# A gated convolution MLP on one core: part of the down projection by seven block products instead of eight

## The chip, the core and the metric

The kernel runs on one core of a Trainium2 chip. The metric is device time of one execution in microseconds. A core has TensorE (PE, matmuls; its weight loads are listed as PEld), VectorE (DVE), ScalarE (ACT), GpSimd (POOL) and SyncE (SP), each working through its own instruction stream, and 16 DMA engines that move data between device memory and the core's SBUF. Matmul results land in PSUM, eight banks of 128 partitions x 512 floats.

## The reference

One layer of a decoder trunk on 256 tokens with 2048 columns, in float32: an attention mixer (latent attention and sliding-window attention, gated and merged), then a gated MLP with a causal convolution of width 3. The change is in the MLP:

```python
D_MODEL = 2048; SEQ = 256; D_FF = 5632; CONV_WIDTH = 3

def conv_ffn(h, w_up, conv_w, conv_b, w_down):
    S = h.shape[1]
    a, b = jnp.split(h @ w_up, 2, axis=-1)
    ap = jnp.pad(a, ((0, 0), (CONV_WIDTH - 1, 0), (0, 0)))
    c = conv_b
    for j in range(CONV_WIDTH):
        c = c + conv_w[j] * ap[:, j:j + S]
    return (jax.nn.gelu(c, approximate=True) * b) @ w_down

x = x + rms_norm(hybrid_mixer(rms_norm(x, norm_mix_pre), ...), norm_mix_post)
x = x + rms_norm(conv_ffn(rms_norm(x, norm_ffn_pre), ...), norm_ffn_post)
```

The down projection is (256 x 5632) times (5632 x 2048).

## The kernel before, in words

**Three matmuls for one.** Every float32 operand is held as a high and a low part, each in the matmul's reduced float format. A product is three matmuls: high x high, high x low, low x high (`mm3`, lines 163 to 166). A matmul has a 128 x 128 stationary operand, here the activations of one ktile (128 values of the inner dimension) and one row tile (128 of the 256 tokens), and a moving operand of up to 512 weight columns.

**How weights come in.** `wchunk` (lines 116 to 140) fetches 512 KB of weights from SP's queue into a raw buffer of 128 x 1024 floats, which is one column block of 512 for two ktiles. ACT then casts it to the high part (line 138), and DVE subtracts to get the low part (line 139). There are three raw buffers in this part of the kernel (`RAW = 3`) and five slots for high and low parts (`RING = 4` and one extra pair that the `flex` buffers supply). `gemm` (lines 168 to 188) loops over the chunks of one column block: two ktiles x two row tiles x three matmuls, 12 matmuls a chunk.

**What sets the order.** The program is written in one order, and small pieces of other work (transposes, gate columns, loads) are put between the chunks with `at(t, f)`: f is written out when the counter `now`, which `tick()` moves on by one a chunk, reaches t. A planner then fixes each engine's order: it takes ready work in the program's order of rank and moves work up where an engine would be idle. It also gives out buffers: a tile of a tag with n buffers waits until the n-th before it is done with.

**The MLP.** The 44 ktiles of the inner dimension D_FF come in 11 column blocks of 512. Block 0 is made by `ffn_up0`, blocks 1 to 10 by `ffn_up` (lines 1007 to 1028): 16 chunks, eight for the activation half into the four PSUM banks of pool `pacc`, eight for the gate half into the four banks of pools `pss` and `pst`. Their results are brought into SBUF by ACT and DVE (`evac`, lines 1011 to 1019), and four `conv_cols` (lines 912 to 926), written among the first seven chunks of what follows, do the convolution, the gelu and the gate, and leave the ktile's 256 tokens as high and low parts (`GH`, `GL`). There is room for 24 ktiles of these. So the down projection has two parts: after block 5 the first 24 ktiles (lines 1036 to 1044), one column block of 512 after the other, each with 12 chunks, into two PSUM banks, which ACT and DVE then copy to `dsum`. Blocks 6 to 10 follow, then the second part with 20 ktiles (lines 1085 to 1106), which adds its results to `dsum`, takes the norm and (`finish`, lines 1071 to 1083) adds x2, the residual stream, in SBUF since the mixer, and stores the output, row tile 0 in four pieces and row tile 1 in five.

**Memory.** x2 lies in SBUF from the mixer's end to the last addition, in two tiles of 128 x 2048 floats (tags `x2_0`, `x2_1`). The results of `evac` lie in tiles of 128 x 512, four each of tags `fa` and `fb`.

Of the kernel before, what the change touches and what calls it, by code (L numbers as in the profile page):

```python
# [19 lines left out]
P = 128  # L20
# [21 lines left out]
def trunk_layer(ctx, tc, x, x_cols_in, conv_cols_in, g_mix_post, g_ffn_post, w_in, w_q, w_kv,  # L42
# [16 lines left out]
    def sb(pl, shape, name, dt=F32, tag=None, bufs=None):  # L59
        return pl.tile(shape, dt, name=name, tag=tag or name, **({"bufs": bufs} if bufs else {}))  # L60
# [55 lines left out]
    def wchunk(src, shape, own=None, rawp=None, rbufs=1, parts=None):  # L116
        i = cnt[0]
        cnt[0] += 1
        n = int(np.prod(shape))
        raw = rawp.tile([P, 1024], F32, name=f"raw{i}", tag="xraw", bufs=rbufs) if rawp else \  # L120
            ring_tile("raw", f"raw{i}", F32, in_turn("raw"))
        dst = raw[:, :n]
        if len(shape) == 2:
            dst = dst.rearrange("p (a b) -> p a b", a=shape[0])
        elif len(shape) == 3:
            dst = dst.rearrange("p (a b c) -> p a b c", a=shape[0], b=shape[1])
        if len(shape) == 3:
            for k in range(shape[0]):
                nc.sync.dma_start(dst[:, k], src[:, k])
        else:  # L130
            nc.sync.dma_start(dst, src)
        if own:
            hi, lo = (own.tile([P, 1024], F32R, name=f"w{part}{i}", tag="w" + part) for part in ("hi", "lo"))
        else:
            extra = in_turn("w")
            hi, lo = (ring_tile("w" + part, f"w{part}{i}", F32R, extra) for part in ("hi", "lo"))
        for a, b in parts or ((0, n),):
            act.copy(hi[:, a:b], raw[:, a:b])  # L138
            vec.tensor_tensor(lo[:, a:b], raw[:, a:b], hi[:, a:b].bitcast(F32), op=ALU.subtract)  # L139
        return hi, lo  # L140


    steps = defaultdict(list)
    now = [0]

    def at(t, *fs):
        steps[max(t, now[0])].extend(fs)
# [444 lines left out]

    ta_d = dram.tile([4, NT, P, 512], F32, name="ta_d")
    yb_d = dram.tile([4, NT, P, 512], F32, name="yb_d")

    def gate_b(j):
        acc, _ = gemm(XH, XL, w_in, 0, KT, C_GB + 512 * j, 512)
# [233 lines left out]
            at(now[0] + (3 if j == 3 else 1) + p, lambda p=2 * j + p, ld=ld: m_cols(p, ld))  # L831


    yg = [[sb(p6, [P, 512], f"yg_{t}_{j}", tag="f" + "ab"[t], bufs=4) for j in range(4)] for t in range(NT)]
# [114 lines left out]
    def ffn_up0():  # L949

        sa = [[None, None], [None, None]]

        def evac(acc, q):
            for t in range(NT):
                a = sb(p6, [P, 512], f"f{q}_0_{t}", tag="f" + "ab"[q], bufs=4)
# [51 lines left out]
    def ffn_up(c, slot0):  # L1007

        sa = [[], []]

        def evac(acc, q):
            for i in range(4):
                if i % 2 == 0:
                    f = sb(p6, [P, 512], f"f{q}_{c}_{i}", tag="f" + "ab"[q], bufs=4)
                a = f[:, (i % 2) * 256:(i % 2) * 256 + 256]
                sc = (1.0, 0.5)[q]
                act.activation(a, acc[i][:, 256:512], AF.Copy, scale=sc)
                vec.scalar_tensor_tensor(a, acc[i][:, 0:256], sc, a, op0=ALU.mult, op1=ALU.add)
                sa[q].append(a)

        acc = [pacc.tile([P, 512], F32, name=f"ua{c}_{i}", tag="acc") for i in range(4)]
        gemm_cols(acc, 512 * c)
        evac(acc, 0)
        acc = [(pss, pst)[i // 2].tile([P, 512], F32, name=f"ub{c}_{i}", tag="st"[i // 2]) for i in range(4)]
        gemm_cols(acc, DFF + 512 * c)
        evac(acc, 1)
        for i in range(4):
            at(now[0] + 1 + 2 * i, lambda i=i: conv_cols(4 * c + i, sa[0][i], sa[1][i], slot0 + i))
# [2 lines left out]
    gpost2 = sb(p6, [P, D], "gpost2", tag="gp")  # L1031
    pool.dma_start(gpost2, g_ffn_post.partition_broadcast(P))
    for c in range(1, 6):
        ffn_up(c, 4 * c)

    def down(k0, nk, c0, n, split=None, ps=None):
# [34 lines left out]
    def finish(t):  # L1071
        v, y, w, r = (sb(p3, [P, 1], f"{n}z{t}") for n in "vywr")
        q = ssz[t][:, NB - 1:NB]
        act.activation(y, q, AF.Sqrt, scale=1.0 / D, bias=zpre[t])
        vec.tensor_scalar(v, q, -0.5 / D, zneg[t], op0=ALU.mult, op1=ALU.add)
        vec.reciprocal(y, y)

        vec.scalar_tensor_tensor(w, v, y[:, 0:1], y, op0=ALU.mult, op1=ALU.mult)
        vec.scalar_tensor_tensor(r, w, 1.5, y, op0=ALU.add, op1=ALU.mult)
        cuts = (0, 256, 768, 1280, 1792, 2048) if t else (0, 512, 1024, 1536, 2048)  # L1080
        for a, b in zip(cuts[:-1], cuts[1:]):
            vec.scalar_tensor_tensor(dsum_all[t][:, a:b], dsum_all[t][:, a:b], r[:, 0:1], x2_all[t][:, a:b], op0=ALU.mult, op1=ALU.add)
            nc.sync.dma_start(out[t * P:(t + 1) * P, a:b], dsum_all[t][:, a:b])
# [104 lines left out]
```

## Time and profile before

| | |
|---|---|
| median of 3 runs | 1477.52 us (1477.09 to 1478.06) |
| the profiled execution, its time | 1477.15 us |
| its span, first to last instruction | 1475.4 us |
| mean granted TensorE clock | 0.998 |
| blocks 1 to 5 of the up projection | 44.5 us each |
| first part of the down projection | 1004.45 to 1135.01 us of the span |
| bytes read from device memory | 275.69 MB |

How to read the rows: a group row is "line engine operation output<-input shape xcount | busy us in all, mean ns of one | idle us of the engine before them, and what ended most of it". Tile names leave their numbers out: `whi` and `wlo` are the weights' high and low parts, `raw` the raw buffer, `accg` a PSUM bank of a `gemm`, `ua` and `ub` the banks of an up block, `ghl` and `bhl` the activations' parts, `ds` the tile of `dsum`. A row of the list of waits is "who, line <- for whom, line: us in all, times, longest". A row of a timeline is "start, duration, engine, line, operation, x count, idle time before it". Lines of helpers (138, 139, 164 to 166, 219, 220) serve many stages.

### The profile page before, as it was taken

To read this page: it belongs to the slowest core of one execution; us is meant where nothing else is said; L and a number is where in the kernel's file an instruction comes from. 1 tells how busy PE (TensorE), PEld (TensorE's weight loads), DVE (VectorE), ACT (ScalarE), POOL (GpSimd) and SP (SyncE) were. 2 spreads that over 40 slices of the span, in tenths; PEclk is the share of its full clock that TensorE was granted. 3 is DMA by queue.
4 is the path that set the end of the run, shared out by engine and by line. 5 is a ranking of instruction groups with operands and counts; after the bars stand their busy time and mean duration, and the time that the engine had idled before them with its cause. 6 is when DMAs were issued, how large, how long until landed. Compare 5 with 4: busy or idle time off the path is not lost.

```text
span 1475.4 us, 20769 instructions
## 1 busy us (share of the span) xinstructions
PE 1464.5 (99%) x7615; PEld 1251.1 (85%) x7615; DVE 979.7 (66%) x1716; ACT 806.2 (55%) x1336; POOL 46.8 (3%) x79
## 2 busy tenths in 40 slices
PE   9999999999999999999999999999999999999997
PEld 7888888888888888888888888888888888888886
DVE  7788874445667665555799677675444676677556
ACT  7588864444565554444666565564444555465443
POOL 0022100000000010000000000000000000000000
PEclk9999999999999999999999999999999999999999
DMA  8755376666655559656656666665656666666663
GB/s 291 219 174 165 94 216 198 204 210 200 186 159 156 171 164 340 223 193 200 194 177 180 197 189 186 189 195 187 198 190 197 188 187 195 188 186 189 197 191 123
DMA packets 159010, 283.40 MB, mean 192 GB/s; under 512 B 18187, under 2 KB 29612, under 8 KB 158780
## 3 DMA queue, kind: packets, MB, share of 16 engines
q1 hardware_dynamic: 154800, 268.34, 59.2%
q0 software_dynamic: 4016, 13.68, 3.1%
q8 instruction: 60, 0.98, 0.3%
q14 instruction: 42, 0.34, 0.1%
q10 hardware_dynamic: 92, 0.05, 0.0%
HBM read 275.69 MB, written 6.34 MB: 191 GB/s over the span
## 4 chain that ended last, share of the span: by engine, by line
PE 96%; DVE 2%; ACT 1%; DMA 1%; issue 0%; DVEq 0%; SPq 0%
PE accg L164 18%; PE accg L166 18%; PE accg L165 18%; PE ub L995 10%; PE ua L995 10%; PE ub L999 5%; PE ua L999 5%; PE mpo L748 1%; PE ms L714 1%; DMA raw<-in_w_in_dram 1%; PE pt L431 1%; PE qn L679 1%; PE qn L677 1%; PE qn L678 1%; PE s L451 0%; PE ms L719 0%
## 5 line engine op out<-in xcount | busy, mean ns | idle before, releaser
L139 DVE TENSOR_TENSOR wlo<-raw,whi 128x1024 fp32r<-128x1024 f32 (+2 forms) x502 | 609.5, 1215 | 404.5 <-ACT whi L138 395.0
L138 ACT CAST whi<-raw 128x1024 fp32r<-128x1024 f32 (+2 forms) x502 | 523.0, 1044 | 513.8 <-PE accg L166 300.8
L164 PE MATMUL accg<-whi,bhl 128*128 128x512 f32 x570 | 222.8, 391 | 0.0
L166 PE MATMUL accg<-whi,bhl 128*128 128x512 f32 x570 | 222.1, 390 | 0.0
L165 PE MATMUL accg<-wlo,bhl 128*128 128x512 f32 x570 | 222.0, 389 | 0.0
L164 PE MATMUL accg<-whi,ahl 128*128 128x512 f32 (+1 forms) x544 | 212.9, 391 | 0.0
L166 PE MATMUL accg<-whi,ahl 128*128 128x512 f32 (+1 forms) x544 | 210.5, 387 | 0.0
L165 PE MATMUL accg<-wlo,ahl 128*128 128x512 f32 (+1 forms) x544 | 209.7, 385 | 0.0
L995 PE MATMUL ua<-ahl,whi 128*128 128x512 f32 x640 | 154.6, 391 | 0.0
L995 PE MATMUL ub<-ahl,whi 128*128 128x512 f32 x640 | 154.5, 391 | 0.0
L995 PEld LDWEIGHTS ub<-ahl,whi 128*128 128x128 f32 x640 | 117.5, 188 | 22.9 <-ACT cc L917 0.2
L995 PEld LDWEIGHTS ua<-ahl,whi 128*128 128x128 f32 x640 | 117.5, 188 | 22.7
L166 PEld LDWEIGHTS accg<-whi,bhl 128*128 128x128 f32 x570 | 107.0, 188 | 22.3
L164 PEld LDWEIGHTS accg<-whi,bhl 128*128 128x128 f32 x570 | 107.0, 188 | 22.0
L165 PEld LDWEIGHTS accg<-wlo,bhl 128*128 128x128 f32 x570 | 107.0, 188 | 21.8
L166 PEld LDWEIGHTS accg<-whi,ahl 128*128 128x128 f32 x544 | 102.1, 188 | 20.4
L165 PEld LDWEIGHTS accg<-wlo,ahl 128*128 128x128 f32 x544 | 102.3, 188 | 18.1
L164 PEld LDWEIGHTS accg<-whi,ahl 128*128 128x128 f32 x544 | 102.3, 188 | 18.0
L999 PEld LDWEIGHTS ub<-ahl,wlo 128*128 128x128 f32 x640 | 82.2, 191 | 3.2
L999 PEld LDWEIGHTS ua<-ahl,wlo 128*128 128x128 f32 x640 | 82.2, 191 | 3.1
L999 PE MATMUL ua<-ahl,wlo 128*128 128x256 f32 x640 | 83.7, 283 | 0.0
L999 PE MATMUL ub<-ahl,wlo 128*128 128x256 f32 x640 | 83.2, 283 | 0.0
(359 smaller groups left out, 1586.5 us busy)
## 6 DMA issues: line engine op xcount, KB each, us to landing
raw<-in_ffn_w_up_dram SPq DMA_DIRECT2D x176, 512.0 KB, 4.4
raw<-in_w_in_dram SPq DMA_DIRECT2D x111, 512.0 KB, 4.5
raw<-in_ffn_w_down_dram SPq DMA_DIRECT2D x88, 512.0 KB, 3.8
raw<-in_w_o_swa_dram SPq DMA_DIRECT2D x32, 512.0 KB, 4.3
raw<-in_w_o_mla_dram SPq DMA_DIRECT2D x32, 512.0 KB, 4.7
raw<-in_w_out_dram SPq DMA_DIRECT2D x32, 512.0 KB, 4.2
bias<-strip POOLq DMA_DIRECT2D x16, 256.0 KB, 4.4
raw<-in_mla_w_q_up_dram SPq DMA_DIRECT2D x32, 128.0 KB, 2.4
```

What stands on the lines that cost most here:

```text
L138: act.copy(hi[:, a:b], raw[:, a:b])
L139: vec.tensor_tensor(lo[:, a:b], raw[:, a:b], hi[:, a:b].bitcast(F32), op=ALU.subtract)
L164: pe.matmul(o, ah, bh, start=start, stop=False)
L165: pe.matmul(o, ah, bl, start=False, stop=False)
L166: pe.matmul(o, al, bh, start=False, stop=stop)
L431: pe.transpose(pt[:, j * P:(j + 1) * P], p[:, c * P:(c + 1) * P], ident)
L677: pe.matmul(o, wh, ch(k), start=k == 0, stop=False)
L678: pe.matmul(o, wh, cl(k), start=False, stop=False)
L679: pe.matmul(o, wl, ch(k), start=False, stop=k == nk - 1)
L714: pe.matmul(o, w, v_, start=n == 0, stop=False)
L995: pe.matmul(acc[i], hi[:, c], hn[p][:, j * 512:(j + 1) * 512], start=p + j == 0, stop=stop)
L999: pe.matmul(acc[i][:, 0:256], lo[:, c], hn[p][:, j * 512:j * 512 + 256], start=False, stop=False)
```

## The change

The first part of the down projection takes two column blocks (1024 columns) at a time, in two halves p = 0 and 1 (`down_pair`), and its ktiles in pairs. A pair, with two row tiles of tokens and two column blocks, is a product of 2 x 2 blocks: eight block products. For pairs 0 to 3 it is done with seven, in Winograd's form of Strassen's method, from sums of blocks: four sums of activation blocks (`token_sums`, made once, used in both halves) and four sums of weight blocks (`ta`, `tb`, made in each half). Pairs 4 to 11 stay plain. The order in a half is `psppsppsppsp` (p plain, s seven).

Each weight row of 128 x 1024 is fetched whole into a raw buffer (`raw_row`); `convert` is the cast and the subtraction of `wchunk`, on their own. A plain pair converts two chunks of 1024. A seven-block converts the odd row (1024), half of the even row (512), `ta` and `tb` (1024 each). Seven products need seven accumulators beside the plain fourth: four banks c11, c12, c21, c22 take what goes to one result block alone, four banks q1, q5, q7, q6 what goes to several; all eight banks are used. After the last seven-block the q banks go into `dsum` by one copy and four additions, and at the half's end the four c banks are added.

The activation sums need room: x2 is stored to device memory (`park`, eight pieces from POOL's queue, written among the chunks of up block 2), its two tiles hold the sums, and x2 is fetched back (`unpark`, eight pieces from SP's queue, placed 40 chunks after the first part). The `fa`/`fb` tiles become 128 x 1024, two of each tag, so that `ta` and `tb` fit in them. Row tile 1 of the output is stored in four pieces of 512, as row tile 0.

```diff
+    def convert(raw, n, own=None, parts=None):
+    def raw_row(src):
+        raw = ring_tile("raw", f"raw{i}", F32, in_turn("raw"))
+        nc.sync.dma_start(raw, src)
+        return raw
...
+    x2_d = dram.tile([NT, P, D], F32, name="x2_d")
...
+    yg_all = [[sb(p6, [P, 1024], f"yg_{t}_{j}", tag="f" + "ab"[t], bufs=2) for j in range(2)] for t in range(NT)]
...
+    def park(t, j):
+        pool.dma_start(x2_d[t, :, j * 512:(j + 1) * 512], x2[t][j])
+
+    def unpark(t, j):
+        if j == 0:
+            x2_all[t] = sb(p3, [P, D], f"x2b_{t}", tag=f"x2_{t}")
+        c = slice(j * 512, (j + 1) * 512)
+        nc.sync.dma_start(x2_all[t][:, c], x2_d[t, :, c])
+
+    def token_sums(u):
+        if u % 2 == 0:
+            s_tiles.append(sb(p3, [P, D], f"s_{u // 2}", F32R, tag=f"x2_{u // 2}"))
+        hi, lo = (s_tiles[u // 2][:, (u % 2) * 1024 + i * 512:(u % 2) * 1024 + (i + 1) * 512] for i in range(2))
+        g = gtiles[u].bitcast(F32)
+        a, m = (sb(s_pool[0], [P, 512], f"s{n}{u}", tag="hx", bufs=2) for n in "am")
+        vec.tensor_tensor(a, g[:, 0:512], g[:, 512:1024], op=ALU.add)
+        a11, a21, a12, _ = (a[:, i * P:(i + 1) * P] for i in range(4))
+        m1, m2, m3, m4 = (m[:, i * P:(i + 1) * P] for i in range(4))
+        vec.tensor_tensor(m1, a21, a[:, 384:512], op=ALU.add)
+        vec.tensor_tensor(m3, a11, a21, op=ALU.subtract)
+        vec.tensor_tensor(m2, m1, a11, op=ALU.subtract)
+        vec.tensor_tensor(m4, a12, m2, op=ALU.subtract)
+        split_to(hi, lo, m)
+        s_of[u] = [[x[:, i * P:(i + 1) * P] for x in (hi, lo)] for i in range(4)]
...
     for c in range(1, 6):
+        if c == 2:
+            for i in range(8):
+                at(now[0] + i, lambda i=i: park(i // 4, i % 4))
+        if c == 4:
+            for u in range(4):
+                at(now[0] + 3 + 3 * u, lambda u=u: token_sums(u))
         ffn_up(c, 4 * c)
...
-    for j in range(4):
-        acc, _ = down(0, 24, 512 * j, 512, ps=(pss, "s") if j == 3 else None)
-        for t in range(NT):
-            vec.tensor_copy(dsum[t][j], acc[t]) if t else act.copy(dsum[t][j], acc[t])
+    def banks(kind, name):
+        return [(pacc if kind == 0 else (pss, pst)[i // 2]).tile([P, 512], F32, name=f"{name}{i}", tag="acc" if kind == 0 else "st"[i // 2])
+                for i in range(4)]
+
+    def down_pair(p):
+        c11, c12, c21, c22 = c = banks(p, f"c{p}_")
+        q1, q5, q7, q6 = q = banks(1 - p, f"q{p}_")
+        j0, used = 2 * p, set()
+        d = [dsum[t][j0 + j] for t in range(NT) for j in range(2)]
...
+        def mul(o, x, w, last=False):
+            mm3(o, *x, *w, id(o) not in used, last)
+            used.add(id(o))
+
+        def plain(u, last):
+            for k in (2 * u, 2 * u + 1):
+                w = convert(raw_row(row(k)), 1024)
+                for t in range(NT):
+                    for j in range(2):
+                        mul(c[2 * t + j], act_of(k, t), half(w, j), last and k % 2 == 1)
+                tick()
+
+        def seven(u, last):
+            s1, s2, s3, s4 = s_of[u]
+            even, odd = raw_row(row(2 * u)), raw_row(row(2 * u + 1))
+            ta, tb = (sb(p6, [P, 1024], f"t{n}{p}_{u}", tag="f" + n, bufs=2) for n in "ab")
+            lo_, hi_ = slice(0, 512), slice(512, 1024)
+            w = convert(odd, 1024)
+            vec.tensor_tensor(ta[:, lo_], even[:, hi_], even[:, lo_], op=ALU.subtract)
+            vec.tensor_tensor(ta[:, hi_], odd[:, hi_], even[:, hi_], op=ALU.subtract)
+            vec.tensor_tensor(tb[:, lo_], odd[:, hi_], ta[:, lo_], op=ALU.subtract)
+            vec.tensor_tensor(tb[:, hi_], odd[:, lo_], tb[:, lo_], op=ALU.subtract)
+            mul(c11, act_of(2 * u + 1, 0), half(w, 0))
+            mul(c12, s4, half(w, 1))
+            w = convert(even, 512)
+            mul(q1, act_of(2 * u, 0), half(w, 0), last)
+            w = convert(ta, 1024)
+            mul(q5, s1, half(w, 0), last)
+            mul(q7, s3, half(w, 1), last)
+            tick()
+            w = convert(tb, 1024)
+            mul(q6, s2, half(w, 0), last)
+            mul(c21, act_of(2 * u + 1, 1), half(w, 1))
+            tick()
+            if last:
+                act.copy(d[0], q1)
+                vec.tensor_tensor(d[1], d[0], q6, op=ALU.add)
+                vec.tensor_tensor(d[2], d[1], q7, op=ALU.add)
+                vec.tensor_tensor(d[3], d[2], q5, op=ALU.add)
+                vec.tensor_tensor(d[1], d[1], q5, op=ALU.add)
+
+        plain_of, seven_of = iter(range(4, 12)), iter(range(4))
+        for i, kind in enumerate(PAIR_ORDER):
+            if kind == "s":
+                u = next(seven_of)
+                seven(u, u == 3)
+            else:
+                plain(next(plain_of), i == len(PAIR_ORDER) - 1)
+        for o, x in zip(d, c):
+            vec.tensor_tensor(o, o, x, op=ALU.add)
+
+    for p in range(2):
+        down_pair(p)
+    for i in range(8):
+        at(now[0] + 40 + 2 * i, lambda i=i: unpark(i // 4, i % 4))
     for c in range(6, 11):
         ffn_up(c, 4 * (c - 6))
...
-        cuts = (0, 256, 768, 1280, 1792, 2048) if t else (0, 512, 1024, 1536, 2048)
+        cuts = range(0, D + 1, 512)
...
+PAIR_ORDER = "psppsppsppsp"
```

More of the change, by code (lines that the diff above doesn't have):

```diff
@@ L131, in wchunk @@
             nc.sync.dma_start(dst, src)
+        return convert(raw, n, own=own, parts=parts)
+    def convert(raw, n, own=None, parts=None):
+        i = cnt[0]
+        cnt[0] += 1
         if own:
@@ L140, in wchunk @@
         return hi, lo
+    def raw_row(src):
+        i = cnt[0]
+        cnt[0] += 1
+        raw = ring_tile("raw", f"raw{i}", F32, in_turn("raw"))
+        nc.sync.dma_start(raw, src)
+        return raw
     steps = defaultdict(list)
@@ L831, in trunk_layer @@
             at(now[0] + (3 if j == 3 else 1) + p, lambda p=2 * j + p, ld=ld: m_cols(p, ld))
-    yg = [[sb(p6, [P, 512], f"yg_{t}_{j}", tag="f" + "ab"[t], bufs=4) for j in range(4)] for t in range(NT)]
+    yg_all = [[sb(p6, [P, 1024], f"yg_{t}_{j}", tag="f" + "ab"[t], bufs=2) for j in range(2)] for t in range(NT)]
+    yg = [[yg_all[t][j // 2][:, (j % 2) * 512:(j % 2 + 1) * 512] for j in range(4)] for t in range(NT)]
     blocks = [(0, 512), (512, 512), (1024, 512), (1536, 256), (1792, 256)]
@@ L953, in evac @@
         def evac(acc, q):
+            f = sb(p6, [P, 1024], f"f{q}_0", tag="f" + "ab"[q], bufs=2)
             for t in range(NT):
-                a = sb(p6, [P, 512], f"f{q}_0_{t}", tag="f" + "ab"[q], bufs=4)
+                a = f[:, t * 512:(t + 1) * 512]
                 act.activation(a, acc[t], AF.Copy, scale=rf[t][q][:, 0:1])
@@ L985, in ffn_up0 @@
             at(now[0] + w, lambda i=i: cols(i))
-        return es7
+        gtiles[:] = g
+        s_pool.append(p7)
+        return es7
+    gtiles, s_pool, s_of = [], [], {}
+    def park(t, j):
[5 more added lines that the diff above has]
+        nc.sync.dma_start(x2_all[t][:, c], x2_d[t, :, c])
+    s_tiles = []
+    def token_sums(u):
[13 more added lines that the diff above has]
+        s_of[u] = [[x[:, i * P:(i + 1) * P] for x in (hi, lo)] for i in range(4)]
     def gemm_cols(acc, c0):
@@ L1011, in evac @@
         def evac(acc, q):
+            f = sb(p6, [P, 1024], f"f{q}_{c}", tag="f" + "ab"[q], bufs=2)
             for i in range(4):
-                if i % 2 == 0:
-                    f = sb(p6, [P, 512], f"f{q}_{c}_{i}", tag="f" + "ab"[q], bufs=4)
-                a = f[:, (i % 2) * 256:(i % 2) * 256 + 256]
+                a = f[:, i * 256:i * 256 + 256]
                 sc = (1.0, 0.5)[q]
@@ L1039, in down @@
         return gemm(xh, xl, w_down, k0, nk, c0, n, split=split, ps=ps)
-    for j in range(4):
-        acc, _ = down(0, 24, 512 * j, 512, ps=(pss, "s") if j == 3 else None)
-        for t in range(NT):
-            vec.tensor_copy(dsum[t][j], acc[t]) if t else act.copy(dsum[t][j], acc[t])
+    def banks(kind, name):
[6 more added lines that the diff above has]
+        d = [dsum[t][j0 + j] for t in range(NT) for j in range(2)]
+        act_of = lambda k, t: (GH(k)[:, t * P:(t + 1) * P], GL(k)[:, t * P:(t + 1) * P])
+        row = lambda k: w_down[k * P:(k + 1) * P, j0 * 512:(j0 + 2) * 512]
+        half = lambda w, i: tuple(x[:, i * 512:(i + 1) * 512] for x in w)
+        def mul(o, x, w, last=False):
[45 more added lines that the diff above has]
+            vec.tensor_tensor(o, o, x, op=ALU.add)
```

## The prediction, made before the change was run

> **What bounds the kernel now.** I read the page first (busy shares, chain), then what TensorE waited for, then the stage of the change.
>
> ```profile
> span 1475.4 us, 20769 instructions
> PE 1464.5 (99%) x7615; PEld 1251.1 (85%) x7615; DVE 979.7 (66%) x1716; ACT 806.2 (55%) x1336; POOL 46.8 (3%) x79
> ...
> PE 96%; DVE 2%; ACT 1%; DMA 1%; issue 0%; DVEq 0%; SPq 0%
> ```
> ```profile
> PE warm L77 <- DVE ramp L66: 1.1, 1, 1.1
> PE pstrip L251 <- DMA sel<-in_strip_sel_dram: 0.5, 1, 0.5
> ```
>
> The second fence is TensorE's whole list of waits, and both are at the start: once going, TensorE is never late by more than a rounding. The chain is TensorE for 96%. A matmul taken out is therefore worth its full pitch, as long as what feeds TensorE keeps up. The pitch comes from the first matmul of the first down part and the first one after it:
>
> ```profile
> 1004.45 0.39 PE L164 MATMUL accg<-whi,bhl 128*128 128x512 f32 x1
> ...
> 1135.01 1.29 PE L995 MATMUL ua<-ahl,whi 128*128 128x512 f32 x5
> ```
>
> Between them lie 4 column blocks x 24 ktiles x 2 row tiles x 3 = 576 matmuls in 130.56 us: 0.2267 us each (the 0.39 of a row overlaps its neighbours and is not the cost). A chunk of weights (one ring slot, 12 matmuls) is 2.72 us, a ktile pair over two column blocks 24 matmuls or 5.44 us.
>
> How far the feed runs ahead is seen in the quiet part of that stage, one conversion on ACT and DVE:
>
> ```profile
> 1015.52 1.05 ACT L138 CAST whi<-raw 128x1024 fp32r<-128x1024 f32 x1 [1.59 <-PE accg L166]
> ```
> ```profile
> 1016.61 1.23 DVE L139 TENSOR_TENSOR wlo<-raw,whi 128x1024 fp32r<-128x1024 f32 x1 [1.39 <-ACT whi L138]
> ```
>
> The cast waited for TensorE to give a slot back: chunk 3 ended at 1004.45 + 4 x 2.72 = 1015.33. There are five slots (RING = 4 and the extra one), so this is chunk 8, which TensorE starts at 1026.2. It is ready at 1017.84, 8.4 us early. That lead is the cover for all that follows.
>
> **What is removed.** In each half (two column blocks) four pairs need 7 products instead of 8: 4 pairs x 2 halves x 3 = 24 matmuls fewer, with their weight loads. 24 x 0.2267 = **5.44 us**. A seven-block has 21 matmuls, 4.76 us. The Trainium skill, "TensorE: Matmul & The Clock Gate", section "Back-to-back issue gap", gives about 131 ns for a 512-column matmul in a stream; by it the sum would be 24 x 0.131 = 3.1 us. The rows of this very stage say 0.2267, and the measurement decides.
>
> **What is added on DVE and ACT in the stage.** Mean durations, of the stage itself and, for shapes it lacks, of the nearest rows elsewhere:
>
> ```profile
> L139 DVE TENSOR_TENSOR wlo<-raw,whi 128x1024 fp32r<-128x1024 f32 x48 | 58.8, 1225 | 63.1 <-ACT whi L138 63.1
> L138 ACT CAST whi<-raw 128x1024 fp32r<-128x1024 f32 x49 | 51.7, 1055 | 70.9 <-PE accg L166 58.0 <-PE accg L165 12.6
> ```
> ```profile
> L722 DVE TENSOR_TENSOR mp<-ms,causal 128x128 f32<-128x128 f32 x16 | 4.6, 286 | 19.6 <-PE ms L719 19.6
> L943 DVE TENSOR_TENSOR hx<-bhl 128x512 f32<-128x512 f32 x8 | 5.4, 683 | 0.0
> ...
> L220 DVE TENSOR_TENSOR ahl<-hx,ahl 128x512 fp32r<-128x512 f32 x8 | 5.3, 683 | 0.0
> L219 ACT CAST ahl<-hx 128x512 fp32r<-128x512 f32 x8 | 4.9, 620 | 3.0 <-DVE hx L945 3.0
> L1055 DVE TENSOR_TENSOR ds<-ds,accg 128x512 f32<-128x512 f32 x6 | 3.8, 679 | 0.0
> ```
>
> A plain pair: 2 subtractions, 2.45 us of DVE for 5.44 of TensorE. A seven-block: 3 conversions of 1024 and one of 512, and four block sums of 512: 3 x 1.225 + 5 x 0.683 = **7.09 us of DVE for 4.76 of TensorE**, and 3 x 1.055 + 0.620 = 3.8 of ACT. So in a seven-block DVE is the slower engine by 2.33 us. In the repeating group (one seven, two plain: 15.64 us of TensorE) DVE has 7.09 + 4.90 = 12.0 us, 77%. On average it fits; the question is whether the lead bridges the block.
>
> A timetable by hand, zero being the start of the two plain pairs ahead of a seven-block (chunks P1 to P4, then O odd row, E even row, T and U the block sums, each in one slot). The slots for O, E, T, U come free at 0, 2.72, 5.44 and 8.16. The rows use three raw buffers, so the odd row is fetched when P3 is converted, at about 0.1, and lands 3.8 us later:
>
> ```profile
> raw<-in_ffn_w_down_dram SPq DMA_DIRECT2D x88, 512.0 KB, 3.8
> ```
>
> O is ready at about 4.5 + 2.3 = 6.8, the first sums at 8.0, the second at 9.2, T at 10.4, U at 11.6. TensorE asks for O at 10.88, E at 12.24, T at 12.92, U at 14.28. The tightest, T and U, are some 2.5 us early. So I expect no wait in the middle of a half. Below, a block could lose nothing; above, with the lead gone, 2.33 us. I take the lower end, because TensorE's list of waits has no entry even where DVE was fuller than here, with 0.3 us in all for eight blocks:
>
> ```profile
> 770.00:780.00 10.00, 10.00 (x46) 8.28 (x45) 9.97 (x14) 5.38 (x7) 0.00 (x0) 1.00 0.71 208
> ...
> 1004.45:1020.77 16.32, 16.32 (x74) 13.51 (x73) 12.25 (x21) 8.90 (x15) 0.00 (x0) 1.00 0.57 190
> 1020.77:1037.09 16.32, 16.32 (x74) 13.51 (x73) 7.35 (x6) 6.81 (x7) 0.00 (x0) 1.00 0.61 194
> ```
>
> (Columns: stretch, PE, PEld, DVE, ACT, POOL busy, clock, DMA share, GB/s.) At 770 DVE is full and PE still 10.00 of 10. The first seven-block comes in the second row's stretch, in which the last gate columns put 12.25 - 7.35 = 4.9 us more on DVE. There the new order has three plain pairs (P, then after the block P, P) and one block: 3 x 2.45 + 7.09 + 4.9 = 19.3 us for 21.1 of TensorE, with four chunks already converted at its start. It fits, more narrowly than the others.
>
> **Results out of PSUM.** Per half, one ACT copy and eight DVE additions (8 x 0.679 = 5.4 us) replace two copies on each; DVE has the room. What waits for them: the four q banks are the next half's c banks, and after the second half the next gate block's. The last seven-block is followed by a plain pair, 5.44 us; from q6's end the evacuation needs 0.6 + 4 x 0.68 = 3.3 us, with one conversion between, 4.5. Hidden; without that pair it would be 3.3 us in each of two places. The c banks have the next half's first pair as cover.
>
> **Block sums of the activations.** Per pair two 512-wide operations, four of 128 and one cast: 2 x 0.683 + 4 x 0.286 = 2.5 us of DVE, 0.62 of ACT; four pairs, 10 us. In the block of columns where they are written, DVE has 44.5 - 31.68 = 12.8 us free and ACT 20:
>
> ```profile
> 915.40:959.90 44.50, 44.50 (x257) 39.35 (x256) 31.68 (x53) 24.08 (x40) 0.00 (x0) 1.00 0.64 189
> ```
>
> They may also go earlier, since the planner pulls ready work ahead: the load of line 1032, written after the first column block, was issued at 738.6. So zero, at worst the 10 us less the lead of 8.4.
>
> **x2 out and back.** Eight stores on POOL's queue, eight loads on SP's, 256 KB each, 4 MB. The rows for one issue on POOL (0.53 us) and one load of x2's size on SP (6.8 us to landing), then a stretch where more of such traffic ran, and what SP waits for in the stage:
>
> ```profile
> L1032 POOL DMA_DIRECT2D gpost<-in_norm_ffn_post_dram x1: 534/534/534, 738.6 to 738.6; - x1
> ```
> ```profile
> x<-in_x_dram SPq DMA_DIRECT2D x8, 256.0 KB, 6.8
> ```
> ```profile
> 560.00:580.00 20.00, 20.00 (x89) 16.54 (x89) 11.41 (x12) 7.79 (x8) 1.08 (x2) 1.00 0.96 341
> ```
> ```profile
> SPq L131 <- DVE wlo L139: 101.9, 45, 2.5
> ```
>
> At 560 the DMA engines were at 0.96 and 341 GB/s and PE had 20.00 of 20, so bursts cost nothing. SP spends 101.9 us of the stage waiting for a raw buffer, so eight more issues find room. A load back waits for the sums' last reader on PE; behind it in SP's queue stand weight rows, and behind these DVE's conversions. It hurts only if it is queued before that reader is done. Fetching weights as whole 4 KB rows moves the same bytes in the same count of loads: no cost.
>
> **The tail.** Each store cut is one DVE operation; four for t = 0 and five for t = 1:
>
> ```profile
> 1462.49 2.74 DVE L1082 SCALAR_TENSOR_TENSOR ds<-ds,rz,x 128x512 f32<-128x512 f32 x4
> ...
> 1468.81 2.87 DVE L1082 SCALAR_TENSOR_TENSOR ds<-ds,rz,x 128x256 f32<-128x256 f32 x5
> ```
> ```profile
> DMA to landing us min/median/max: 1.9/2.4/2.6
> ```
> ```profile
> out_dram<-ds SPq DMA_DIRECT2D x7, 256.0 KB, 2.4
> ...
> out_dram<-ds SPq DMA_DIRECT2D x2, 128.0 KB, 2.2
> ```
>
> Four instead of five saves 0.13 on DVE; the last store is 256 KB, not 128, by the medians 0.2 slower: +0.1 (ends -0.13 and, 1.9 to 2.6, +0.57).
>
> **Sum.** The profiled execution took 1477.15 us (span 1475.4). 1477.15 - 5.44 + 0.3 + 0.1 = 1472.1; the median of the runs is 0.37 above that execution, so **1472.4**.
>
> **Rivals.**
> (1) *The blocks come a little late.* The lead of 2.5 us is worked out with median landings; a DVE queue whose order puts an evacuation or a gate column ahead of T costs 0.4 to 1.0 us a block. For: DVE goes from 47% of the stage (24 x 1.225 + 2 x 0.69 per 65.3) to about 85% (53.4 of 62.6). Against: no wait in the whole run of before. At 0.65 a block in place of the 0.3 in all, 1472.4 - 0.3 + 5.2 = 1477.3, no change.
> (2) *Slower: DVE paces every seven-block.* The sums pin the even and odd raw buffers until the last sum is made, the next rows are fetched late, and the lead doesn't come back in the two plain pairs. Then each block costs its full 2.33 us: 8 x 2.33 = 18.6, so 1477.5 - 5.4 + 18.6 + 0.1 = 1490.8. It decides from 0.67 us a block (break even). Against it: the group's DVE load of 77%.
> (3) *A load of x2 blocks SP.* Queued one group too early, it holds the weight rows for 15.6 us against a lead of 8.4: 7.2 us once, 1479.6, still no change.
> (4) *The matmuls taken out are worth less than their pitch*: at 131 ns each the time is 1474.8. By that rule of the skill; the pitch measured in the stage leaves it next to no chance.
>
> **Chances.** Forecast 0.66 (1471.6 to 1474.5: all blocks hidden, up to 0.3 us each lost). (1) 0.15, (2) 0.13, (3) 0.04, (4) 0.02. A measurement of this kernel tells 0.2%, 3 us, from no change: faster 0.66, same 0.21 (rivals 1, 3, 4), slower 0.13. The range runs from all hidden with the best tail, 1471.5, up through rival 1 to 1478.5, which holds about 8 in 10; the forecast's own is 1471.6 to 1474.5.
>
> **What the profile after would show.** 24 matmuls fewer and 125.1 us instead of 130.6 from the first matmul of the stage to the next gate block; no PE waits there (step "added" right), or waits on the conversions of T and U (rivals 1 and 2), about 0.5 or over 2 us each. DVE at about 85% in the stage. PE waiting at the start of the second half or of the next gate block would show the PSUM step wrong; SP idle on a TensorE releaser, rival 3. PE waiting at 915 to 960 would show the activation sums dear. A pitch other than 0.227 in the seven-blocks would break the first term.

## The result, and the profile after

| | before | after |
|---|---|---|
| median of 20 runs each | 1477.24 us (1476.38 to 1478.21) | 1475.05 us (1473.28 to 1475.86) |
| ratio after / before | | 0.9984, 95% interval 0.9977 to 0.9991 |
| profiled execution: time, span | 1477.15, 1475.4 us | 1475.35, 1473.5 us |
| first matmul of the stage | 1004.45 us | 1003.91 us |
| first matmul of the next gate block (up block 6) | 1135.01 us | 1132.44 us |
| the stage between them | 130.56 us | 128.53 us |
| start of the last matmul to the end of the span | 8.92 us | 8.39 us |

The kernel is faster by 2.2 us. The prediction was 1472.4, a gain of 5.1. The sign is right and the time lies in the whole range (1471.5 to 1478.5), but outside the forecast's own (1471.6 to 1474.5): less than half of the gain came. The page of the profile after:

```profile
span 1473.5 us, 20861 instructions
...
PE 1460.6 (99%) x7591; PEld 1246.1 (85%) x7591; DVE 1026.6 (70%) x1799; ACT 818.3 (56%) x1354; POOL 51.1 (3%) x87
...
PE 92%; DVE 3%; DMA 3%; ACT 1%; issue 0%; DVEq 0%; ACTq 0%; SPq 0%
```

TensorE has 24 matmuls fewer (7615 to 7591), as intended. The last row, the chain, went from 96% on PE to 92%: for some stretch something else sets the end. TensorE's whole list of waits (for whom: us in all, times, longest) says where:

```profile
PE c L176 <- DVE wlo L144: 1.6, 2, 0.8
PE warm L77 <- DVE ramp L66: 1.1, 1, 1.1
PE ua L1041 <- DVE ds L1145: 0.9, 1, 0.9
PE pstrip L262 <- DMA sel<-in_strip_sel_dram: 0.4, 1, 0.4
PE q L176 <- DVE wlo L144: 0.2, 1, 0.2
```

`warm` and `pstrip` are the old waits at the start. New are waits for low parts of weights (`wlo`) in the stage, and one of 0.9 for line 1145, the last addition that takes a q bank out of PSUM. The stage in four parts, two to a half (stretch, PE, PEld, DVE, ACT, POOL busy, clock, DMA share, GB/s):

```profile
1003.91:1035.20 31.29, 31.29 (x140) 25.91 (x139) 24.70 (x35) 16.46 (x23) 0.00 (x0) 1.00 0.57 179
1035.20:1066.47 31.27, 31.27 (x140) 25.89 (x138) 25.34 (x29) 15.96 (x17) 0.00 (x0) 1.00 0.64 202
1066.47:1099.40 32.93, 31.93 (x139) 25.57 (x138) 23.50 (x27) 15.10 (x16) 0.00 (x0) 1.00 0.59 182
1099.40:1132.44 33.04, 32.24 (x140) 25.92 (x139) 24.64 (x27) 16.08 (x18) 0.00 (x0) 1.00 0.69 217
```

The first half takes 62.56 us, which is 276 matmuls x 0.2267: nothing is lost in it. The second half, with the same work, takes 65.97: **3.4 us lost**. With the 0.9 behind it that makes 4.3, where the prediction had 0.3. (The list names 1.8 us in the stage, and these rows show as much idle time, 32.93 - 31.93 and 33.04 - 32.24; the other 1.6 lies in longer steps between matmuls whose ends are modelled, so I go by their starts.) DVE is at 71 to 81% in these rows, so it isn't full. What does set the pace is in the chain of work that ended last, here from the turn of the halves (the end of the first and the start of the second) on (start, duration, what):

```profile
1065.72 0.24 PE c L177
...
1067.20 1.28 DVE ds L1155 x2
1068.47 1.14 DVE wlo L144
...
1070.82 0.60 DVE tb L1126
...
1072.02 0.61 DVE tb L1127
...
1072.65 6.30 DMA raw<-in_ffn_w_down_dram
...
1081.38 5.63 DMA raw<-in_ffn_w_down_dram
...
1087.03 0.69 DVE ta L1125
...
1090.12 3.82 DMA raw<-in_ffn_w_down_dram
...
1096.38 5.74 DMA raw<-in_ffn_w_down_dram
...
1105.80 5.27 DMA raw<-in_ffn_w_down_dram
...
1113.51 6.00 DMA raw<-in_ffn_w_down_dram
...
1122.63 4.02 DMA raw<-in_ffn_w_down_dram
...
1133.54 0.61 DVE ds L1145
...
1134.20 1.42 PE ua L1041 x5
```

Most of the loss can be read in this view. The chain leaves TensorE at 1066, when the first half's last c matmul releases the additions of line 1155. DVE works in order, so the block sums of the second half's first block stand behind these additions. The last sum, at 1072.63, gives a raw buffer back, and from there the chain doesn't return to TensorE until 1134.20: it goes round one raw buffer, load, cast and subtraction (or sums), load again. Six rounds from 1072.65 to 1122.63 take 49.98 us. One buffer of three carries every third row, so six rounds are 18 rows or three groups, for which TensorE needs 3 x 15.64 = 46.92. The difference, 3.06 us, is nearly all of the 3.4 lost. The loads on this chain take 3.8 to 6.3 us, not the 3.8 of the timetable. By the starts of TensorE's matmuls the 3.4 us are lost in two places: 1.8 by 1090, the other 1.6 from 1120.7 on.

What ScalarE waited for in the stage tells the same (before, by the row shown above, it waited for TensorE to give slots back, 58.0 and 12.6 us):

```profile
ACT whi L143 <- DMA raw<-in_ffn_w_down_dram: 52.2, 27, 5.5
...
DVE ta L1125 <- DMA raw<-in_ffn_w_down_dram: 9.4, 6, 2.8
...
ACT whi L143 <- PE c L177: 4.4, 5, 1.5
```

Before, the conversions ran ahead until all slots were full; after, they wait for rows. The stage went from one with a full queue of conversions to one that takes each row as it lands.

### The profile page after: what moved, and what is told of

The parts are those of the page before. It is cut to its first block, busy times and chain, and to the rows that moved or that the text cites. A ratio compares the mean times of both kernels' runs of the same rounds, so it can differ in the third digit from the quotient of the medians.

```text
span 1473.5 us, 20861 instructions
## 1 busy us (share of the span) xinstructions
PE 1460.6 (99%) x7591; PEld 1246.1 (85%) x7591; DVE 1026.6 (70%) x1799; ACT 818.3 (56%) x1354; POOL 51.1 (3%) x87
## 4 chain that ended last, share of the span: by engine, by line
PE 92%; DVE 3%; DMA 3%; ACT 1%; issue 0%; DVEq 0%; ACTq 0%; SPq 0%
PE accg L175 15%; PE accg L177 15%; PE accg L176 15%; PE ub L1041 10%; PE ua L1041 10%; PE ua L1045 5%; PE ub L1045 5%; DMA raw<-in_ffn_w_down_dram 2%; PE c L175 1%; PE c L176 1%; PE c L177 1%; DVE wlo L144 1%; PE mpo L760 1%; PE ms L726 1%; PE pt L442 1%; PE qn L691 1%
## 5 line engine op out<-in xcount | busy, mean ns | idle before, releaser
L175 PE MATMUL accg<-whi,bhl 128*128 128x512 f32 x442 | 173.0, 391 | 0.0
L177 PE MATMUL accg<-whi,bhl 128*128 128x512 f32 x442 | 172.3, 390 | 0.0
L176 PE MATMUL accg<-wlo,bhl 128*128 128x512 f32 x442 | 172.2, 390 | 0.0
L177 PEld LDWEIGHTS accg<-whi,bhl 128*128 128x128 f32 x442 | 83.0, 188 | 17.4
L175 PEld LDWEIGHTS accg<-whi,bhl 128*128 128x128 f32 x442 | 83.0, 188 | 16.9
L176 PEld LDWEIGHTS accg<-wlo,bhl 128*128 128x128 f32 x442 | 83.0, 188 | 16.8
```

The costliest lines, as they stand in the source:

```text
L175: pe.matmul(o, ah, bh, start=start, stop=False)
L176: pe.matmul(o, ah, bl, start=False, stop=False)
L177: pe.matmul(o, al, bh, start=False, stop=stop)
```

## The experiments

**Theory 1**: the three raw buffers are too few for rows that the sums hold longer and that land later; the lead of the feed is used up and can't be won back. **Theory 2**: DVE's load or order (sums, evacuations ahead of conversions). **Theory 3**: the loads of x2, which the planner had moved from 40 chunks behind the stage into its second half (SP issued four of the eight in pairs from 1096.89 and 1101.41, the others after 1131), crowd the weight rows.

A measure for them is the lead of a block: the time from the end of the subtraction that gives the low part of T (U) to the matmul that first reads it (eight, for U two, pitches of 0.2267 before the end of the block's last q matmul). About 0.2 us is the least it can be; there TensorE waits. The stage began between 1003.80 and 1006.58 in the profiled executions, of kernels that are mostly alike up to it. So stages are compared by length, from the first matmul in them to the first of the next gate block, and times by medians. Each ratio is to the kernel before, run on the same chip.

### no_seven: everything but the seven-blocks

```diff
-PAIR_ORDER = "psppsppsppsp"
+PAIR_ORDER = "pppppppppppp"
```

All twelve pairs are plain, c goes straight to `dsum`. The sums of activations, x2 out and back, whole rows and the tail stay.

> The changed kernel with all twelve pairs plain in both halves (576 matmuls, as before the change), so that the activation sums are made but not used, the q banks are not used, and the results are copied out of the c banks. All theories: PE has no wait in the stage, 130.6 us. It shows what the rest of the change costs by itself: against the kernel before, the output tail and nothing else, so 0 to 1 us less. Theory 1 also: whole rows land in about 3.8 to 4.0 us when each buffer is held for a conversion only. If whole rows are slow by themselves, they land in 4.3 or more here too.

1476.84 us (1475.77 to 1477.47), ratio 0.9997 (0.9988 to 1.0006); the stage is 130.56 us, as before, without a wait. What the change brings with it costs nothing that can be told, as long as the blocks don't use up the feed.

### tail_only and tail_only_timed: the kernel before, row tile 1 stored in four pieces

```diff
-        cuts = (0, 256, 768, 1280, 1792, 2048) if t else (0, 512, 1024, 1536, 2048)
+        cuts = range(0, D + 1, 512)
```

> The kernel before with nothing but the four output pieces for row tile 1. From the end of the last matmul to the end of the span it took 8.9 us before and 8.4 in the changed kernel. If the pieces are the reason, 8.4 here; if something else of the change is, 8.9.

> The kernel before with only the output's last rows stored in four equal pieces instead of five. From the last matmul to the end it took 8.4 us in the one look, against 8.92 before: if that holds, 1477.25 - 0.5 = 1476.7, a ratio of 0.9997. By the prediction's term (+0.1, ends -0.13 and +0.57) 1477.1 to 1477.8.

A single execution took 1478.76 us, its first stages 2 us late; from the last matmul to the end 1477.0 - 1468.60 = 8.4. The median of eleven is 1476.35 (1476.05 to 1477.49), ratio 0.9997 (0.9988 to 1.0006), and 1474.2 - 1465.82 = 8.4 again. The change has 8.39, the kernel before 8.92. So the tail gains about 0.5 us, in three traces against one; in the times it can't be told from nothing. In the changed kernel the last additions and the eight stores are

```profile
1467.45 2.74 DVE L1198 SCALAR_TENSOR_TENSOR ds<-ds,rz,x2b 128x512 f32<-128x512 f32 x4
```
```profile
DMA to landing us min/median/max: 2.0/2.1/2.2
```

0.13 on DVE came as worked out. The rest is between the last issue and the end of the span: 1471.7 to 1475.4 before, 1470.2 to 1473.5 after, 3.7 against 3.3. The bigger last store was not the slower one.

### gp_raw: the block's rows in buffers of their own

```diff
-            even, odd = raw_row(row(2 * u)), raw_row(row(2 * u + 1))
+            even, odd = own_row(row(2 * u), 0), own_row(row(2 * u + 1), 1)
```

`own` is the 8 KB of the output's gain, which is loaded after the stage instead.

> The changed kernel with two more weight-row buffers for the seven-blocks alone: the even and odd rows land in the 8 KB that the output gain holds, and the gain is loaded after the first down part. DVE, ACT and PE have the same work. Theory 1 (three raw buffers are too few: a seven-block pins two of them until its sums are made, so the next rows are asked for late): the waits of the second half go, the stage takes 125.1 to 125.6 us instead of 128.5 and the wait of the next gate block goes with them, the time is 3 to 5 us under that of the changed kernel. Theory 2 (DVE's own load and order): the waits stay at 3 to 4.5 us, the time within 1 us of the changed kernel. Theory 3 (the loads of x2 crowd the rows): the first wait, at 1076 to 1090, goes or stays as in theory 2, the one at 1122 and the one of the gate block stay, 1 to 2 us.

1480.43 us, ratio 1.002 (1.0011 to 1.003): **slower** than before. The stage took 1141.18 - 1005.56 = 135.6 us. Two rows of its list of waits in the stage:

```profile
DVE ta L1122 <- DMA own<-in_ffn_w_down_dram: 24.1, 6, 6.1
...
PE c L176 <- DVE wlo L144: 5.3, 5, 1.4
```

Two buffers more, and worse. There is only one pair for the blocks, so its load starts when the block before is done with its rows, and the planner put the next sums early in DVE's queue: DVE stood 24.1 us for rows that had not landed, with conversions that were ready behind the wait. Theory 1 failed in this form, but the form changed two things: buffers and order. It didn't settle the matter; it showed what it costs when an in-order engine is made to wait on a late load.

### late_x2 and late_x2_timed: the loads of x2 held back

```diff
-        nc.sync.dma_start(x2_all[t][:, c], x2_d[t, :, c])
+        tc.keep_in_program_order(nc.sync.dma_start(x2_all[t][:, c], x2_d[t, :, c]))
```

The call keeps the load at its written place in SP's order.

> The changed kernel with the eight loads of x2 held at their place in the program, 40 chunks after the first down part, instead of being moved up by the planner. Theory 3: the waits at the end of the second half and at the next gate block go, 2 us of 4.3, and rows land a microsecond sooner from 1097 on. Theories 1 and 2: the waits at 1076 to 1090 stay as they are, the others shrink by less than 1 us, the stage still takes 127.5 us or more.

> The changed kernel with the x2 loads held at their written place, 40 chunks behind the down stage, now timed. It lost 3.4 us in the second half of the stage and 0.9 at the next gate block in its profiled execution. If the x2 loads between the weight rows are what made the second half late (theory 3), all of the 3.4 us come back in every run: 1475.05 - 3.4 = 1471.7, a ratio to the kernel before of 0.9963. If three raw buffers are too few whatever else is in the queue (theory 1), the lead of the block sums still falls from 4 us to under 0.5 us over eight blocks, the second half loses 1 to 3 us in some executions, and the median lies between 1473 and 1475. If DVE's order is the cause (theory 2), nothing changes: 1475.

A single execution took 1473.64 us, its stage 1130.68 - 1005.30 = 125.38, with no wait in it, though 1.0 behind it. That spoke for theory 3. The median of ten is 1474.02 us (1473.08 to 1475.19), ratio 0.9979 (0.997 to 0.9988), which overlaps that of the changed kernel, and their profiled execution has the stage at 1130.66 - 1004.20 = 126.46 with these waits among others:

```profile
PE ua L1041 <- DVE ds L1145: 0.9, 1, 0.9
PE q L176 <- DVE wlo L144: 0.4, 1, 0.4
```

Not all of the 3.4 us came back, and the lead ran out as before (table below). The chain that ended last goes round one raw buffer here too, from

```profile
1073.59 5.30 DMA raw<-in_ffn_w_down_dram
...
1096.10 5.42 DMA raw<-in_ffn_w_down_dram
...
1120.76 4.08 DMA raw<-in_ffn_w_down_dram
```

on: six rounds in 47.17 us, 7.86 each, where TensorE takes 7.82 for the three rows of a round (46.92 / 6) and the changed kernel's rounds took 8.33 (49.98 / 6). The rounds are shorter by the loads, 5.0 us on average instead of 5.5; the rest of a round is 2.9 in both. Of the 2.8 us between the two chains 1.2 lie in the first three rounds, before any x2 load was issued in the changed kernel, so they are scatter; 1.6 lie in the last three, among the x2 loads. So the x2 loads are a part of the loss, about 1 us by the medians (not resolved) and up to 1.6 in the profiles. They aren't the whole of it: the 1.8 us lost by 1090 came before them, and without them the ring is still at its edge, 7.86 against 7.82.

### ring5_late, ring4_late: five and four buffers in one ring

```diff
-        raw = ring_tile("raw", f"raw{i}", F32, in_turn("raw"))
+        i, h = cnt[0], nth[0] % 5 - 3
+        raw = ring_tile("raw", f"raw{i}", F32, in_turn("raw")) if h < 0 else hold[0][:, h * 1024:(h + 1) * 1024]
```

(% 4 for four.) All rows, plain and seven, go round the ring; the two places come from the gain's tile, which is loaded behind the stage. x2 loads as in late_x2.

> As late_x2, but the weight rows go through five buffers instead of three (the two more lie in the 8 KB of the output gain, which is loaded after the stage). Theory 1 (too few buffers): with 5 x 15.64 / 6 = 13 us a row instead of 7.8, against a load of 4 to 6 and a hold of 2.3 to 3.0, the lead of T and U over their use no longer falls from block to block, is over 2 us at the eighth block, and there is no wait on conversions in the stage: 125.1 us, and 1471.7 in time, or 1472.7 if the wait for the evacuation behind the stage (1.0) stays. Theory 2 (DVE's order or load): the lead falls as before, 4 to under 1 us, and the time is that of late_x2. If five rows ahead crowd the DMA engines, landings grow from 4 to over 6 us and the first gate blocks show waits for rows.

> Four buffers for the weight rows: 4 x 15.64 / 6 = 10.4 us a row, between the 7.8 of three and the 13.0 of five; a row of sums takes 4 to 6 us to land and is held 3. Theory 1: the lead of the blocks lies between the two, 1.5 to 4 us away from the turn of the halves, no waits but up to 0.4 us at the turn, and the time is ring5_late's, 1472.6 within 0.7. If it is like late_x2 (lead under 1 us at the end, 1474.0), it wasn't the count of buffers but the two whole pairs of own rows that helped.

Five: 1472.57 us (1471.36 to 1473.14), ratio 0.9966 (0.9953 to 0.9978), stage 1129.45 - 1003.99 = 125.46. Four: **1471.80** us (1470.96 to 1472.1), ratio 0.9964 (0.9951 to 0.9976), stage 1130.06 - 1004.67 = 125.39; this interval lies wholly below that of the changed kernel. TensorE's list has no entry for either stage, and none behind it (the 0.3 us over 125.12 are short delays at the turn, too short for the list). ScalarE's waits in the stage of ring5_late:

```profile
ACT whi L143 <- PE c L177: 24.1, 19, 2.1
...
ACT whi L143 <- DMA raw<-in_ffn_w_down_dram: 8.9, 5, 2.5
...
ACT whi L143 <- DMA own<-in_ffn_w_down_dram: 5.7, 2, 2.9
```

It waits for TensorE again, 24.1 us, and for rows 14.6 instead of 52.2. The lead (the smaller of T's and U's, us; blocks 1 to 4 in the first half, 5 to 8 in the second):

| kernel | block 1 | 4 | 5 | 6 | 8 |
|---|---|---|---|---|---|
| after | 3.8 | 1.5 | 0.2 | 0.5 | 0.2 |
| late_x2_timed | 3.8 | 0.8 | 0.2 | 0.5 | 0.3 |
| ring4_late | 3.8 | 2.9 | 0.2 | 3.5 | 2.8 |
| ring5_late | 3.8 | 1.5 | 1.3 | 3.8 | 3.8 |
| no_c_half1 (below) | 3.8 | 1.1 | 1.8 | 1.8 | 1.7 |

With three buffers the lead sinks through the first half, and in the first two rows what is lost at the turn (block 5) doesn't come back. With four it falls at the turn just as low, costs 0.3 us there once, and is back a block later. Theory 1 holds: with 4 x 15.64 / 6 = 10.4 us a row the ring has room over the 7.86 us that a round took without the x2 loads and over the 8.33 with them; with three, 7.82, it has none.

### ring5: five buffers, the x2 loads where the planner puts them

It is ring5_late without the line that holds the loads back.

> Five buffers, with the x2 loads where the planner puts them, in the stage among the weight rows as in the changed kernel. If they hurt only because the rows had no lead left, this costs nothing against ring5_late: 1472.6 within 0.7. If they hurt by themselves (they fill the DMA engines or hold SP's queue), 1 us or more as between the changed kernel and late_x2: 1473.6 to 1476.

1472.45 us (1471.31 to 1472.96), ratio 0.9967 (0.9954 to 0.9979), against 1472.57 with them held back; stage 125.12 us. Six of the x2 loads were issued in this stage. With a feed that has a lead they cost nothing; theory 3 needs a feed without one.

### late_order and ring5_late_order: two plain pairs at the end of a half

```diff
-PAIR_ORDER = "psppsppsppsp"
+PAIR_ORDER = "psppsppspspp"
```

> As late_x2 with the pairs of each half in the order p s p p s p p s p s p p: the last seven-block is followed by two plain pairs instead of one, and two blocks stand one plain pair apart instead of two. If the wait of 0.9 to 1.0 us at the next gate block is the evacuation of q out of PSUM (DVE, four additions after q6), it goes: 1.0 us less than late_x2 in time. By theory 1 the two close blocks need their S rows 5.4 us sooner than the ring gives them back with a lead under 1 us: a wait of 2 to 5 us ahead of the fourth and the eighth block, and the time is 1 to 6 us over late_x2. By theory 2 the wait there is about the 2.3 us by which a block's DVE work is over its PE work, once or twice.

> Both: five buffers and the order with two plain pairs at the end. Theory 1: the close blocks are covered by the two more buffers, the wait at the next gate block is gone and there is none in the stage: 125.1 us for it, 1.0 us less than ring5_late, about 1470.7 to 1471.5. Theory 2: the waits ahead of the fourth and eighth block stay at about 2 us each, as in late_order.

late_order: 1473.17 us (1472.1 to 1474.87), ratio 0.9972 (0.9961 to 0.9982). The wait of 0.9 at the next gate block is gone, but not the loss in the second half (the stage takes 126.56), whose one wait in TensorE's list is

```profile
PE c L176 <- DVE wlo L144: 0.7, 1, 0.7
```

The 1 to 6 us that theory 1 foresaw for the two close blocks didn't come, and the reason is arithmetic: a block and one plain pair use 4 rows in 10.2 us, 2.55 us a row, a group 6 in 15.64, 2.61. Close blocks ask hardly more of the ring. ring5_late_order: **1471.49** us (1470.99 to 1473.06), ratio 0.9961 (0.9947 to 0.9974), the lowest median of all, though not to be told apart from ring4_late. Both beat the kernel before and the changed one. Its stage was foreseen at 125.1 without a wait; in the profiled execution it took 125.81, with a wait of 0.2 for a conversion of a plain pair (1109.6), which no run here explains.

### no_c_half1: without the additions at the turn

```diff
-        for o, x in zip(d, c):
+        for o, x in (zip(d, c) if p else ()):
```

late_x2 with the four c additions of the first half left out, so that half of the output lacks these partial sums.

> As late_x2, but the first half's four c results aren't added into the partial sums (the first 1024 output columns lack them; 4 x 0.62 = 2.48 us of DVE work left out at the turn of the halves, no other engine's work changed). In every kernel with three buffers the first block of the second half had the same small lead, 1.07 us for T and 0.16 for U, whatever the lead before. If that is DVE's backlog of the two evacuations (q 2.75 us and c 2.48 us, standing in its queue ahead of the sums), the lead there grows by about 2.5 us, to 3 us or more, the following blocks lose it at the 0.8 us a block of the first half, and no wait for a conversion stands in the second half: 125.1 us and the wait of 0.9 behind the stage. If the buffers alone set it (raw rows fetched late), it stays near 1.07 and 0.16.

1471.68 us (1470.5 to 1473.35), ratio 0.9965 (0.9952 to 0.9978). Three buffers, and yet TensorE waits nowhere in the stage or at its end: 1129.29 - 1004.17 = 125.12 us, which is 552 x 0.2267. The whole list, both entries from ahead of the stage:

```profile
PE warm L77 <- DVE ramp L66: 1.1, 1, 1.1
PE ub L1041 <- DVE uu L938: 0.3, 1, 0.3
```

2.48 us of DVE's work taken out at the turn, in a stage where DVE isn't full, took out both losses of late_x2_timed, 1.3 us in the stage and 0.9 behind it; that the second would go too wasn't foreseen. The lead at block 5 rose to 1.8, less than the 3 expected, and then didn't sink by 0.8 a block: 1.8, 1.8, 2.3, 1.7. So three buffers can hold a small lead, but in none of these runs do they build up one like that of four: what was foreseen as a steady loss ends at a floor. Theory 2 has its part: the additions in DVE's queue are what drops the lead below it.

## Why the prediction was half right

- **Removed: 24 x 0.2267 = 5.44 us.** Right. Without waits the stage is 125.12 us (ring5, no_c_half1) against 130.56, 5.44 less. By the 131 ns of the Trainium skill ("TensorE: Matmul & The Clock Gate", section "Back-to-back issue gap") it would have been 3.1; rival 4 is out, and that its 1474.8 us is the nearest to the measured time is chance.
- **Added on DVE in a block, and the timetable: "no wait in the middle of a half", 0.3 us in all.** This is the step that failed. The DVE durations were right (0.68 and 1.22 in the rows of the stage), though as costs they are too high: in a row of operations the next one starts 1.14 us after a long one and 0.60 after a short one (1129.27 to 1130.41 and 1132.86 to 1133.46 below), so a block is 3 x 1.14 + 5 x 0.60 = 6.4 us of DVE and not 7.09, and the stage's 85% came out as 71 to 81. For the first half the conclusion held too. But the timetable took a landing of 3.8 us for every row, and treated each block alone, with its lead coming back in the plain pairs. It doesn't: the lead sinks from 3.8 to 1.5 us over the first half. The loads of the chain took 5.5 us on average and up to 6.3, a round 8.33 (7.86 without the x2 loads) against the 7.82 that three buffers allow. It costs 3.4 us in the second half.
- **Results out of PSUM: "DVE has the room ... hidden".** Also wrong, and it is what sets off the first. As work the additions fit; the text asked what waits for the banks, and not what stands behind the additions on DVE. They can't begin before TensorE ends the half, so DVE, however far ahead, comes back to TensorE's time there, and the sums of the next block wait behind them. After the second half the late feed does the reverse. The text allowed one conversion behind q6's end. In the changed kernel that end is at about 1126.3 (twelve q matmuls from 1123.28 on), and DVE's timeline there is

```profile
1127.84 1.23 DVE L144 TENSOR_TENSOR wlo<-raw,whi 128x1024 fp32r<-128x1024 f32 x1 [1.27 <-ACT whi L143]
1129.27 1.23 DVE L144 TENSOR_TENSOR wlo<-raw,whi 128x1024 fp32r<-128x1024 f32 x1 [0.20 <-ACT whi L143]
1130.41 0.68 DVE L1142 TENSOR_TENSOR ds<-ds,q 128x512 f32<-128x512 f32 x1
...
1131.73 1.22 DVE L144 TENSOR_TENSOR wlo<-raw,whi 128x1024 fp32r<-128x1024 f32 x1
1132.86 0.68 DVE L1144 TENSOR_TENSOR ds<-ds,q 128x512 f32<-128x512 f32 x1
1133.46 0.68 DVE L1145 TENSOR_TENSOR ds<-ds,q 128x512 f32<-128x512 f32 x1
```

  Three conversions, two of them standing for late rows, make the evacuation end 7.8 us after q6 and not 4.5, and TensorE waits 0.9. Where the feed has a lead (ring4_late, ring5_late, no_c_half1) it is hidden, as the text had it.
- **Activation sums: zero; stores of x2: zero; whole rows: zero.** Right by no_seven in time. The sums were moved up, and TensorE's list has no wait there.
- **Loads of x2: zero.** Right with a lead (ring5); without one about 1 us by the medians, not resolved, and up to 1.6 in the profiles.
- **Tail: +0.1.** The measured -0.5 is outside the ends given.
- **Sum.** Of the profiled execution: 4.0 more than the 0.3 for the stage and its end, 0.63 less for the tail, 0.54 less for a stage that began earlier by chance, 0.3 more in the gate blocks behind, and 0.1 more outside the span: 1472.1 + 3.2 = 1475.3, as measured.
- **Rivals.** What came was rival 1 in size (it had 5.2 us of loss, 4.3 came) by the cause that rival 2 named: "the next rows are fetched late, and the lead doesn't come back in the two plain pairs". Rival 2 priced that cause by DVE's 2.33 us a block; the price is that of the raw ring, 0.04 us a round without the x2 loads and 0.5 in the changed kernel, once the turn has taken the lead. The DVE load of 77% that spoke against it was no evidence, since DVE was not what ran out.

## What to carry to other kernels

Price a feed by its ring: buffers x time per row the bottleneck needs, against landing plus hold, with landings as they are when rows are bunched, and not as the median of a quiet stage. In these runs a feed at the edge at best kept the small lead that it had, so look for the point that takes the lead away: an in-order engine that must wait for the bottleneck's last result (an evacuation) ahead of the work that feeds its next one. Either change was enough here with the x2 loads held back, one more buffer or fewer instructions at that point (with five buffers they needn't be held back). The second was tried by leaving out additions that the output needs, so it shows the cause and is no cure as it stands. A low busy share of the engine was no evidence that its order doesn't matter.

## What the hardware showed that I had not expected

The same 512 KB landed later as the stage changed, at the same traffic (189 to 191 GB/s in the three). Median landings of the loads issued in the first 62 us of the stage, in the kernel before, in no_seven and in the changed kernel:

```profile
raw<-in_ffn_w_down_dram SPq DMA_DIRECT2D x22, 512.0 KB, 3.8
```
```profile
raw<-in_ffn_w_down_dram SPq DMA_DIRECT2D x22, 512.0 KB, 4.2
```
```profile
raw<-in_ffn_w_down_dram SPq DMA_DIRECT2D x22, 512.0 KB, 4.4
```

Whole 4 KB rows in half as many packets (3216 in no_seven against 6078, on all queues in that stretch) were not faster to land. That they were 0.4 us slower holds for this stretch alone: from 1066 to 1125 the three medians are 3.7, 3.8 and 4.6. The blocks' pairs of rows come with 0.2 us more in the first stretch and 0.8 in the second, which holds x2 loads as well; late_x2_timed, without them, has 4.6 and 4.3. That two rows under way at once share the engines would explain the longer landings; it was not tried by itself.
